# Slot tables read behind the first expert's activation, expert numbers loaded one by one, down biases issued behind the next up

## The chip, the core and the metric

The kernel runs on one core of a Trainium2 chip. Its engines work side by side, each with its own queue in program order: TensorE (PE: matmuls and transposes), VectorE (DVE), ScalarE (ACT), GpSimd (POOL) and SyncE (SP). SP issues the large weight transfers, POOL those with computed row addresses. An instruction starts when those ahead of it on its engine are done and the semaphores it waits for are up. The metric is the device time of one execution in microseconds (us). The kernel before takes 1528.14 us (median of 3 runs, 1527.29 to 1529.5).

## The reference

One decoder layer for 512 tokens of width 1024, in fp32: a normalised input projection feeds a retention and a sliding-window attention group, whose results go through an output projection and are added to `h`. Then comes the part that the change touches, a mixture of experts:

```
logits = xf @ w_router + b_router                 # 512 tokens x 32 experts
top_v, top_i = lax.top_k(logits, 4);  gate = softmax(top_v)
h_e = xblk @ w_up[e] + b_up[e]                    # 1024 -> 2048, tokens grouped by expert
y_e = clamped_swiglu(h_e) @ w_down[e] + b_down[e] # 1024 -> 1024
h   = h + sum over a token's 4 experts of gate * y_e
```

A gated per-layer embedding and a last norm end the layer. Every expert's weights (8 MB up, 4 MB down) are read once; all 32 are used.

## The kernel before

**Routing.** After the router each token has four (expert, position) pairs. Experts are sorted on the chip by their number of tokens and run in a fixed pattern of 32 slots: 20 "L" slots of up to 96 tokens and 12 "S" slots of up to 64, in the order LL SLLSL (five times) SLLLS. For the first two experts `route` (which uses matmuls) builds the row lists at once. For the other thirty, 16 indirect transfers on POOL (L982, four for each of the four tables `slot_d[k]`) scatter token numbers and gates into DRAM, by slot; the table rows are then read back and summed:

```
for k in range(4):                                               # L1005
    nc.gpsimd.dma_start(out=tab[0:CAP, k, :], in_=slot_d[k]...)
R.slots = nc.vector.tensor_reduce(out=slots..., in_=tab...)      # L1006
nc.gpsimd.dma_start(out=slots[64:P, NBIG:E, :], in_=slots[0:64, NBIG:E, :])   # L1008
```

L1009 to L1012 make from it `slot_i`, the row numbers by which `gather` (L798) fetches an expert's tokens and `scatter` (L929) adds its result into `acc`. All this stands in the program between `any_blk` (L1001) and the expert loop.

**Expert loop.** In step e the order of the code is: the gather for expert e+2; `up` or `up64` of expert e (8 pieces of weights); `act` (ACT L885, DVE L886 and L887); the transposes of expert e+1's tokens (`prep` or `prep64`, which make `xTh` and, by DVE L290, `xTl`); `down` of expert e-1 (4 pieces), its gated copy `y` (L924) and its scatter; the transposes of the activation, `act_t` (L901) or `act_t64` (L812). A scheduler orders each engine's queue from this by what is ready; `tc.issue_after(x)` tells it to put an instruction behind `x`.

**L and S.** An L piece (1 MB) is split in two: ACT copies it into `wh` (L150) and DVE subtracts to get `wl` (L151, two operands from SBUF); three products wh·xTh, wh·xTl and wl·xTh (L841) make fp32 precision. An S piece goes to the matmuls unsplit (L858). The bias of a product is a small matmul of its own: `add_bias` (L829) for L, `bias64` (L851) for S. For a down it opens the accumulation.

**Weights.** `next_piece` and `whole_piece` hand out pieces in one fixed order; 12 rotating `raw` tiles hold them, and SP issues the next transfer (L184 up, L189 down) when a tile comes free. Since experts are sorted on the chip, each transfer's address comes from a register, loaded by SP from `eid_i` (`expert_of`, L179). The scheduler put all 30 register loads side by side on SP, ahead of the third up piece.

Of the kernel before, what the change touches and what calls it, by code (L numbers as in the profile page):

```python
# [22 lines left out]
P = 128  # L23
S = 512
NT = S // P
D = 1024
# [69 lines left out]
def hymba_kernel(ctx, tc, x, p, positions, rel_bias_table, g_mix_norm, w_in, b_in, ret_norm_g,  # L96
# [76 lines left out]
    def expert_of(w, t):  # L173

        if t < 2:
            return w[t]
        if t not in R.eid:
            r = RANK[t]
            R.eid[t] = nc.values_load(R.eid_i[0:1, r:r + 1], engines=[mybir.EngineType.SP], min_val=0, max_val=E - 1)  # L179
        return w[bass.ds(R.eid[t], 1)].rearrange("o k c -> (o k) c")  # L180

    def w_up_piece(e, k):
        def load(t):
            nc.sync.dma_start(out=t, in_=expert_of(w_up, e)[k * P:(k + 1) * P, :])  # L184
        return load

    def w_down_piece(e, f):
        def load(t):
            nc.sync.dma_start(out=t.rearrange("p (k c) -> p k c", k=2),  # L189
                              in_=expert_of(w_down, e)[f * 2 * P:(f + 1) * 2 * P, :].rearrange("(k p) c -> p k c", p=P))  # L190
        return load

    def w_proj_piece(t):
# [38 lines left out]
    def whole_piece(use):  # L232

        t, pl_ = queue.pop(0)
        use(t)
        free.append(pl_)
        prefetch()
# [586 lines left out]
    def add_bias(o, e, c0, n, **kw):  # L824

        for c in range(0, n, 512):
            for v in range(2):
                rows = slice(v * 64, v * 64 + 64)
                nc.tensor.matmul(o[v][:, c:c + 512], lhsT=sel[rows, RANK[e]:RANK[e] + 1].broadcast_to([64, P]),  # L829
                                 rhs=R.bias[rows, c0 + c:c0 + c + 512], **kw)  # L830

    def up_tile():
        return R.up.tile([P, 1024], F32, name="up")
# [1 line left out]
    def up(xT, piece, e):  # L835
        h = [up_tile(), up_tile()]
        for k in range(KD):
            wh, wl = piece(k)
            for a, w in ((xT[0], wh), (xT[1], wh), (xT[0], wl)):
                for n in range(4):  # L840
                    nc.tensor.matmul(h[n // 2][:, n % 2 * 512:n % 2 * 512 + 512], lhsT=a[:, k, :],  # L841
                                     rhs=w[:, n * 512:(n + 1) * 512], start=(k == 0 and a is xT[0] and w is wh), stop=False)
        add_bias(h, e, 0, 1024, start=False, stop=True)
        return h

    def bias64(o, e, c0):
# [6 lines left out]
    def pairs64(o, xT, k, w, last):  # L853

        n = w.shape[1] // 2
        for c in range(0, n, 512):
            for v in range(2):
                nc.tensor.matmul(o[v * 64:v * 64 + 64, c:c + 512], lhsT=xT[:, k, :], rhs=w[:, v * n + c:v * n + c + 512],  # L858
                                 start=False, stop=last, tile_position=(0, v * 64))

    def up64(xT, e):
        h = up_tile()
        bias64(h, e, 0)
        for k in range(KD):
            whole_piece(lambda w: pairs64(h, xT, k, w, k == KD - 1))
        return [h]

    def down64(aT, e):
        o = R.dn.tile([P, D], F32, name="dn")[:, 0:512]
        bias64(o, e, 1024)  # L870
        for f in range(4):
            def use(w):
                for kk in range(2):
                    pairs64(o, aT, f * 2 + kk, w[:, kk * D:(kk + 1) * D], f * 2 + kk == KD - 1)
            whole_piece(use)
        return o
# [30 lines left out]

    def down(aT, piece, e):
        o = R.dn.tile([P, D], F32, name="dn")
        add_bias([o[:, 0:512], o[:, 512:D]], e, 1024, 512, start=True, stop=False)  # L910
        for f in range(4):
            wh, wl = piece(f)
            for kk in range(2):
                k = f * 2 + kk
                for a, w in ((aT[0], wh), (aT[1], wh), (aT[0], wl)):
                    for n in range(2):
                        nc.tensor.matmul(o[:, n * 512:(n + 1) * 512], lhsT=a[:, k, :],  # L917
                                         rhs=w[:, kk * 1024 + n * 512:kk * 1024 + (n + 1) * 512],
                                         start=False, stop=(k == KD - 1 and w is wl))
        return o  # L920
# [79 lines left out]
    any_blk = rt.tile([P, 1], I32, name="any_blk")  # L1000
    nc.vector.tensor_copy(out=any_blk, in_=nb_m)  # L1001

    tab = tl.tile([P, 4, 2 * E], F32, name="tab", bufs=1)
    for k in range(4):
        nc.gpsimd.dma_start(out=tab[0:CAP, k, :], in_=slot_d[k].rearrange("(s e) c -> s (e c)", e=E))  # L1005
    R.slots = nc.vector.tensor_reduce(out=slots.rearrange("p e c -> p (e c)")[0:CAP], in_=tab[0:CAP].rearrange("p k f -> p f k"),  # L1006
                                      op=ALU.add, axis=AX.X)
    nc.gpsimd.dma_start(out=slots[64:P, NBIG:E, :], in_=slots[0:64, NBIG:E, :])  # L1008
    nc.vector.tensor_scalar(slot_i[0:CAP, 0:NBIG], slots[0:CAP, 0:NBIG, 0], 512.0, None, op0=ALU.add)  # L1009
    half = tl.tile([P, E], F32, name="cmp", bufs=1)[:, NBIG:E]  # L1010
    nc.vector.tensor_scalar(half, slots[:, NBIG:E, 0], 2.0, 1024.0, op0=ALU.mult, op1=ALU.add)
    nc.vector.tensor_scalar(slot_i[:, NBIG:E], half, cst[:, C_HALF:C_HALF + 1], None, op0=ALU.add)  # L1012
    px.close()

    def open_pools(stack, tag, dn=True):
# [18 lines left out]
    for e in range(E + 1):  # L1034
        if e < E:
            def piece(k, e=e):
                if ahead:
                    return ahead.pop(0)
                with tc.issue_after(R.act.ins) if (e, k) == (1, 2) else nullcontext():
                    return next_piece()  # L1040

            if e + 2 < E:
                static_gather(e + 2)
            h = up(xT, piece, e) if BIG[e] else up64(xT, e)
            a = act(h)
            if e + 1 < E:
                xT = (prep if BIG[e + 1] else prep64)(xe[(e + 1) % 2])
        if e == E - 1:

            last = raw_tile()  # L1050
            aT_last = act_t64(a)
        if e == E:
            tmp = raw_tile()
            p_sb = tmp[0][:, 0:D].rearrange("p (i d) -> p i d", i=NT)
            nc.sync.dma_start(out=p_sb, in_=p.rearrange("(i p) d -> p i d", p=P))
            state["limit"] = n_moe + 3
            for _ in range(3):
                prefetch(after=y)
            ph, pl = halves(raw_tile(F32R)[0], 2)
            for i in range(NT):  # L1060
                split_t(R.tp, p_sb[:, i, :], ph[:, :, i * P:(i + 1) * P], pl[:, :, i * P:(i + 1) * P], n=2)
            aT = aT_last
        if e > 0:
            big = BIG[e - 1]
            y = gated(down(aT, lambda f: next_piece(), e - 1) if big else down64(aT, e - 1), routes[e - 1][1])
            scatter(y, routes[e - 1][0], CAP if big else P, 1 if big else 2)
        if e < E - 1:
            aT = act_t(a) if BIG[e] else act_t64(a)
# [184 lines left out]
```

## Time and profile before

| | |
|---|---|
| median of 3 runs | 1528.14 us |
| profiled execution, its own time | 1529.3 us |
| its span, first to last instruction | 1527.2 us |
| busy: PE, DVE, ACT, POOL | 1379.6, 888.4, 728.7, 209.9 us |
| mean granted TensorE clock | 0.962 of full |
| L150 splits on ACT (267), mean | 1863 ns |
| L151 splits on DVE (267), mean | 2229 ns |
| weights over q1 | 436.24 MB, 73.2% of 16 engines' span |

The span is what the trace covers; the execution's own time is 2.1 us longer. Busy time is a sum over stages: PE is busy for 90% of the span; the experts run from about 303 to 1440 us, and PE stands still from about 307 to 333 us. A time in a row counts from the start of the span.

### The profile page before, as it was taken

The numbers are of one execution on the slowest core, as the hardware profiler recorded it, in microseconds if no ns is written. First come the engines' busy times: TensorE is split into PE (matmuls) and PEld (weight loads), VectorE is DVE, ScalarE is ACT, GpSimd is POOL, SyncE is SP. The second block draws the span as 40 slices with busy tenths as digits, with TensorE's granted clock in tenths as the row PEclk, the third lists the DMA queues.
The fourth block names the chain that finished last, engine by engine and source line by source line (L and its number), as shares of the span: only waits on it lengthen the run. The fifth ranks groups of instructions, "written<-read, shape, count | busy, mean of one in ns | idle before, by whom it ended". The sixth has DMA issues, their size and how long they took to land. (4 is left out here: it accounts for less than half of the span.)

```text
span 1527.2 us, 17227 instructions
## 1 busy us (share of the span) xinstructions
PE 1379.6 (90%) x6208; PEld 939.0 (61%) x6209; DVE 888.4 (58%) x1052; ACT 728.7 (48%) x782; POOL 209.9 (14%) x230
## 2 busy tenths in 40 slices
PE   6998999529999999999999999999999999999785
PEld 4775777427677647656567647656567647675464
DVE  6535674728576537656366627646366537684256
ACT  5333543416465526544455516544355526564343
POOL 2203231450111100000100100000100100000013
PEclk9998999759999999999999999999999999999898
DMA  8422146618899999999999999999999999996601
GB/s 258 136 83 56 36 149 257 235 61 327 328 397 407 380 411 398 407 380 386 397 392 362 375 395 399 403 326 387 395 390 356 375 388 411 387 346 251 215 23 52
DMA packets 110428, 462.49 MB, mean 303 GB/s; under 512 B 10954, under 2 KB 29304, under 8 KB 77568
## 3 DMA queue, kind: packets, MB, share of 16 engines
q1 hardware_dynamic: 99584, 436.24, 73.2%
q0 software_dynamic: 10320, 24.51, 6.3%
q8 instruction: 50, 0.82, 0.2%
q10 hardware_dynamic: 432, 0.57, 0.1%
q14 instruction: 42, 0.34, 0.1%
HBM read 447.53 MB, written 18.99 MB: 305 GB/s over the span
## 5 line engine op out<-in xcount | busy, mean ns | idle before, releaser
L151 DVE TENSOR_TENSOR wl<-raw,wh 128x2048 fp32r<-128x2048 f32 (+2 forms) x267 | 585.4, 2229 | 124.9 <-ACT wh L150 113.7
L150 ACT ACTIVATE wh<-raw 128x2048 fp32r<-128x2048 f32 (+2 forms) x267 | 489.3, 1863 | 129.2 <-PE up L841 90.5
L841 PE MATMUL up<-wh,xTl 128*128 128x512 f32 x640 | 178.3, 400 | 26.7 <-DVE xTl L290 26.7
L841 PE MATMUL up<-wh,xTh 128*128 128x512 f32 x640 | 179.1, 401 | 7.8 <-ACT wh L150 6.3
L841 PE MATMUL up<-wl,xTh 128*128 128x512 f32 x640 | 179.5, 402 | 2.3 <-DVE wl L151 2.3
L858 PE MATMUL up<-raw,xTh 128*64 128x512 f32 x768 | 169.4, 595 | 0.0
L886 DVE TENSOR_SCALAR a<-up 128x512 f32<-128x512 f32 x52 | 34.0, 686 | 232.5 <-ACT sg L885 232.5
L841 PEld LDWEIGHTS up<-wh,xTl 128*128 128x128 f32 x640 | 121.7, 190 | 56.7 <-DVE xTl L290 27.4
L841 PEld LDWEIGHTS up<-wl,xTh 128*128 128x128 f32 x640 | 119.9, 190 | 43.4 <-issue 8.4
L841 PEld LDWEIGHTS up<-wh,xTh 128*128 128x128 f32 x640 | 119.5, 189 | 41.5 <-ACT wh L150 11.6
L798 POOL DMA_INDIRECT xe<-xg,slot_i x30 | 40.6, 1354 | 565.4 <-PE tp L298 317.1
L858 PEld LDWEIGHTS up<-raw,xTh 128*64 128x64 f32 x768 | 53.2, 137 | 103.3 <-issue 98.2
L885 ACT ACTIVATE sg<-up 128x512 f32<-128x512 f32 x52 | 28.9, 598 | 165.7 <-PE up L858 84.2
L917 PE MATMUL dn<-wl,aTh 128*128 128x512 f32 x320 | 103.8, 406 | 4.2 <-DVE wl L151 4.2
L917 PE MATMUL dn<-wh,aTh 128*128 128x512 f32 x320 | 105.6, 412 | 0.3 <-ACT wh L150 0.3
L929 POOL DMA_INDIRECT acc<-y,slot_i x30 | 45.1, 1504 | 419.8 <-ACT y L924 409.8
L917 PE MATMUL dn<-wh,aTl 128*128 128x512 f32 x320 | 102.7, 403 | 0.0
L858 PE MATMUL dn<-raw,aT 128*64 128x512 f32 x384 | 100.1, 601 | 0.0
L924 ACT ACTIVATE y<-dn,slots 128x1024 f32<-128x1024 f32 (+1 forms) x30 | 28.3, 944 | 102.2 <-PE dn L917 81.9
L917 PEld LDWEIGHTS dn<-wl,aTh 128*128 128x128 f32 x320 | 59.8, 192 | 21.0 <-DVE wl L151 8.0
L917 PEld LDWEIGHTS dn<-wh,aTh 128*128 128x128 f32 x320 | 59.5, 193 | 18.9 <-ACT wh L150 2.8
L917 PEld LDWEIGHTS dn<-wh,aTl 128*128 128x128 f32 x320 | 61.5, 192 | 15.0
(338 smaller groups left out, 1566.9 us busy)
## 6 DMA issues: line engine op xcount, KB each, us to landing
raw<-in_w_up_dram SPq DMA_DIRECT2D x256, 1024.0 KB, 11.4
raw<-in_w_down_dram SPq DMA_DIRECT2D x128, 1024.0 KB, 11.0
raw<-in_w_in_dram SPq DMA_DIRECT2D x32, 256.0 KB, 4.8
raw<-in_w_out_dram SPq DMA_DIRECT2D x4, 1024.0 KB, 5.7
raw<-in_w_ple_gate_dram SPq DMA_DIRECT2D x4, 1024.0 KB, 12.4
raw<-in_w_in_dram SPq DMA_DIRECT2D x3, 1024.0 KB, 5.3
xt<-in_x_dram SPq DMA_DIRECT2D x4, 512.0 KB, 7.4
h<-in_x_dram POOLq DMA_DIRECT2D x4, 512.0 KB
```

What stands on the lines that cost most here:

```text
L150: R.split_act = nc.scalar.activation(to(wh), src(raw), AF.Copy)
L151: R.split_dve = nc.vector.tensor_tensor(out=to(wl), in0=src(raw), in1=to(wh).bitcast(F32), op=ALU.subtract)
L798: return nc.gpsimd.indirect_dma_start(out=dst[0:n, 0:D // h], out_offset=None, in_=xg.rearrange("s (h d) -> (s h) d", h=h), in_offset=bass ...
L841: nc.tensor.matmul(h[n // 2][:, n % 2 * 512:n % 2 * 512 + 512], lhsT=a[:, k, :], rhs=w[:, n * 512:(n + 1) * 512], start=(k == 0 and a is x ...
L858: nc.tensor.matmul(o[v * 64:v * 64 + 64, c:c + 512], lhsT=xT[:, k, :], rhs=w[:, v * n + c:v * n + c + 512], start=False, stop=last, tile_p ...
L885: nc.scalar.activation(sg[:, cs], hv[:, :, 0], AF.Silu, scale=ALPHA)
L886: nc.vector.tensor_scalar(a[:, cs], hv[:, :, 1], LIMIT + 1.0, 1.0 - LIMIT, op0=ALU.min, op1=ALU.max)
L917: nc.tensor.matmul(o[:, n * 512:(n + 1) * 512], lhsT=a[:, k, :], rhs=w[:, kk * 1024 + n * 512:kk * 1024 + (n + 1) * 512], start=False, sto ...
L924: nc.scalar.activation(y[:, 0:o.shape[1]], o, AF.Copy, scale=gate)
L929: nc.gpsimd.indirect_dma_start(out=acc.rearrange("s (h d) -> (s h) d", h=h), out_offset=bass.IndirectOffsetOnAxis(ap=idx[0:n, :], axis=0), ...
```

## The change

Three parts. (1) The reading of the slot tables becomes a function `read_slots`, called in step 0 of the expert loop behind `act`; its reduction is put behind the activation's last DVE instruction, `R.act`. The gather for expert 2 moves behind it. Its two scratch tiles are now buffers of the loop's `y`. (2) Each register load of an expert number is put behind the last weight transfer issued before it. (3) The bias matmuls of a down are put behind the last matmul of the up that precedes it in the program (`R.up_end`).

```
@@ expert_of
-            R.eid[t] = nc.values_load(R.eid_i[0:1, r:r + 1], engines=[mybir.EngineType.SP], min_val=0, max_val=E - 1)
+            with tc.issue_after(R.load.ins):
+                R.eid[t] = nc.values_load(R.eid_i[0:1, r:r + 1], engines=[mybir.EngineType.SP], min_val=0,
+                                          max_val=E - 1)
@@ w_up_piece (w_down_piece alike)
-            nc.sync.dma_start(out=t, in_=expert_of(w_up, e)[k * P:(k + 1) * P, :])
+            R.load = nc.sync.dma_start(out=t, in_=expert_of(w_up, e)[k * P:(k + 1) * P, :])
@@ up: add_bias now returns its last matmul
-        add_bias(h, e, 0, 1024, start=False, stop=True)
+        R.up_end = add_bias(h, e, 0, 1024, start=False, stop=True)
@@ up64: pairs64 keeps its last matmul in R.pair
+        R.up_end = R.pair
@@ down64
-        bias64(o, e, 1024)
+        with tc.issue_after(R.up_end.ins):
+            bias64(o, e, 1024)
@@ down
-        add_bias([o[:, 0:512], o[:, 512:D]], e, 1024, 512, start=True, stop=False)
+        with tc.issue_after(R.up_end.ins):
+            add_bias([o[:, 0:512], o[:, 512:D]], e, 1024, 512, start=True, stop=False)
@@ behind any_blk
-    tab = tl.tile([P, 4, 2 * E], F32, name="tab", bufs=1)
-    for k in range(4):
-        nc.gpsimd.dma_start(out=tab[0:CAP, k, :], in_=slot_d[k].rearrange("(s e) c -> s (e c)", e=E))
-    R.slots = nc.vector.tensor_reduce(...)
-    ...
+    def read_slots():
+        tab = R.sb.tile([P, D], F32, name="y")[:, 0:8 * E].rearrange("p (k f) -> p k f", k=4)
+        half = R.sb.tile([P, D], F32, name="y")[:, NBIG:E]
+        for k in range(4):
+            nc.gpsimd.dma_start(out=tab[0:CAP, k, :], in_=slot_d[k].rearrange("(s e) c -> s (e c)", e=E))
+        with tc.issue_after(R.act.ins):
+            nc.vector.tensor_reduce(...)
+        ...
@@ expert loop
-            if e + 2 < E:
+            if 0 < e < E - 2:
                 static_gather(e + 2)
             h = up(xT, piece, e) if BIG[e] else up64(xT, e)
             a = act(h)
+            if e == 0:
+                read_slots()
+                static_gather(2)
```

VectorE's queue from the end of the routing to the second expert's first split, before (`tab` is what POOL reads back from the slot tables; the first `xTl` pair belongs to expert 0, the second to expert 1):

```order
L1001 CAST any_blk<-nb_m 128x1
L1006 TENSOR_REDUCE slots<-tab 96x64
L1009 TENSOR_SCALAR slot_i<-slots 96x20
L1011 TENSOR_SCALAR cmp<-slots 128x12
L1012 TENSOR_SCALAR slot_i<-cmp,cst 128x12
L290 TENSOR_TENSOR xTl<-tp,xTh 128x512 x2
L151 TENSOR_TENSOR wl<-raw,wh 128x2048 x8
L886 TENSOR_SCALAR a<-up 128x512 x2
L887 SCALAR_TENSOR_TENSOR a<-sg,a 128x512 x2
L290 TENSOR_TENSOR xTl<-tp,xTh 128x512 x2
L151 TENSOR_TENSOR wl<-raw,wh 128x2048
L904 SCALAR_TENSOR_TENSOR aTl<-tp,aTh 128x512 x2
```

The same stretch after the change (`y` is the tile into which the tables are now read, and the scratch of L1020):

```order
L1007 CAST any_blk<-nb_m 128x1
L292 TENSOR_TENSOR xTl<-tp,xTh 128x512 x2
L151 TENSOR_TENSOR wl<-raw,wh 128x2048 x8
L891 TENSOR_SCALAR a<-up 128x512 x2
L892 SCALAR_TENSOR_TENSOR a<-sg,a 128x512 x2
L1016 TENSOR_REDUCE slots<-y 96x64
L292 TENSOR_TENSOR xTl<-tp,xTh 128x512
L1019 TENSOR_SCALAR slot_i<-slots 96x20
L292 TENSOR_TENSOR xTl<-tp,xTh 128x512
L151 TENSOR_TENSOR wl<-raw,wh 128x2048
L1020 TENSOR_SCALAR y<-slots 128x12
L909 SCALAR_TENSOR_TENSOR aTl<-tp,aTh 128x512
```

The reduction and the three small instructions behind it moved past expert 0's `xTl`, its eight splits and its activation; they now stand in front of and between the two `xTl` of expert 1.

TensorE's queue at the end of the up of expert 12, an S slot (its products are `up<-raw`; `tp<-cst,a` are the transposes of its activation, the products behind them the down of expert 11, whose bias is `dn<-bias`), before:

```order
L298 MATMUL tp<-cst,xe_2055 128x128 x4
L829 MATMUL dn<-bias,sel 128x512 x2
L858 MATMUL up<-raw,xTh 64x512 x32
L812 MATMUL tp<-cst,a 128x128 x4
L298 MATMUL tp<-cst,xe_2054 128x128
L917 MATMUL dn<-wh,aTh 128x512 x2
L917 MATMUL dn<-wh,aTl 128x512 x2
```

And after the change:

```order
L300 MATMUL tp<-cst,xe_2055 128x128 x8
L861 MATMUL up<-raw,xTh 64x512 x32
L831 MATMUL dn<-bias,sel 128x512 x2
L814 MATMUL tp<-cst,a 128x128 x4
L300 MATMUL tp<-cst,xe_2054 128x128
L923 MATMUL dn<-wh,aTh 128x512 x2
L923 MATMUL dn<-wh,aTl 128x512 x2
```

The two bias matmuls moved from ahead of the 32 up products to behind them, just ahead of the transposes that wait for the activation. In five L slots that follow an L slot (experts 9, 14, 19, 24 and 29) the bias moves in the same way from ahead of the up to behind it; in the S slots 10, 15, 20, 25 and 31 it moves there from the middle of the up. In S slot 5 the transposes of the activation now stand ahead of the down products and not among them. On SP one register load stands ahead of each expert's first piece, where all thirty stood together.

## Rows read from the trace of the kernel before

**Rows 1.** Waits from 307 to 1440 us: total, times, longest.
```profile
PE up L841 <- DVE xTl L290: 26.7, 1, 26.7
...
PE up L841 <- ACT wh L150: 6.3, 5, 1.3
...
PE dn L829 <- ACT y L924: 1.8, 9, 0.2
```

**Rows 2.** Windows: PE, PEld, DVE, ACT, POOL busy; clock; DMA share; GB/s.
```profile
480.00:530.00 50.00, 50.00 (x234) 33.06 (x233) 29.81 (x22) 26.41 (x23) 9.13 (x5) 1.00 1.02 387
...
333.50:337.10 3.60, 3.58 (x9) 2.81 (x9) 2.76 (x2) 1.47 (x1) 1.09 (x1) 0.50 0.23 68
337.10:340.00 2.90, 2.90 (x14) 2.36 (x13) 2.29 (x1) 1.26 (x2) 0.00 (x0) 0.99 0.90 288
```

**Rows 3.** Timeline 300 to 337 us: start, duration, instruction, [idle before <-releaser].
```profile
305.95 1.04 POOL L982 DMA_INDIRECT slot_d<-pay,dest  x1 [7.48 <-DVE dest L979]
...
306.78 0.15 DVE L1001 CAST any_blk<-nb_m 128x1 int32<-128x1 f32 x1
...
325.20 0.97 POOL L982 DMA_INDIRECT slot_d<-pay,dest  x1 [0.30 <-issue]
...
329.83 0.58 DVE L1006 TENSOR_REDUCE slots<-tab 96x64 f32<-96x256 f32 x1 [22.89 <-DMA tab<-slot_d]
330.44 0.17 DVE L1009 TENSOR_SCALAR slot_i<-slots 96x20 int32<-96x20 f32 x1
...
332.77 1.29 DVE L290 TENSOR_TENSOR xTl<-tp,xTh 128x512 fp32r<-128x512 f32 x2
...
333.52 2.07 PE L841 MATMUL up<-wh,xTl 128*128 128x512 f32 x4 [26.68 <-DVE xTl L290]
```

**Rows 4.** Timeline of DVE, 333 to 364 us: expert 0's splits and activation.
```profile
333.98 2.28 DVE L151 TENSOR_TENSOR wl<-raw,wh 128x2048 fp32r<-128x2048 f32 x1
337.58 2.29 DVE L151 TENSOR_TENSOR wl<-raw,wh 128x2048 fp32r<-128x2048 f32 x1 [1.31 <-ACT wh L150]
...
355.13 2.29 DVE L151 TENSOR_TENSOR wl<-raw,wh 128x2048 fp32r<-128x2048 f32 x1 [0.51 <-ACT wh L150]
...
359.61 1.28 DVE L887 SCALAR_TENSOR_TENSOR a<-sg,a 128x512 f32<-128x512 f32 x2
```

**Rows 5.** Timeline of DVE at 385 us.
```profile
385.18 2.29 DVE L151 TENSOR_TENSOR wl<-raw,wh 128x2048 fp32r<-128x2048 f32 x1 [0.51 <-ACT wh L150]
```

**Rows 6.** Timeline of POOL at 385 us.
```profile
385.64 2.66 POOL L798 DMA_INDIRECT xe<-xg,slot_i  x1 [25.80 <-PE tp L812]
```

**Rows 7.** Timeline of all engines, 796 to 798 us.
```profile
796.06 1.59 POOL L929 DMA_INDIRECT acc<-y,slot_i  x1 [0.31 <-issue]
796.40 2.29 DVE L151 TENSOR_TENSOR wl<-raw,wh 128x2048 fp32r<-128x2048 f32 x1 [2.92 <-ACT wh L150]
```

**Rows 8.** Timeline of POOL, 290 to 300 us.
```profile
293.43 2.78 POOL L798 DMA_INDIRECT xe<-xg,idx  x1 [0.85 <-DVE idx L793]
```

**Rows 9.** Timeline of PE, 293 to 340 us.
```profile
301.76 0.90 PE L298 MATMUL tp<-cst,xe 128*128 128x128 f32 x3 [8.45 <-DMA xe<-xg,idx]
```

**Rows 10.** Timeline of PE, 660 to 752 us.
```profile
669.47 0.49 PE L829 MATMUL dn<-bias,sel 64*128 64x512 f32 x2
669.90 7.09 PE L858 MATMUL up<-raw,xTh 128*64 128x512 f32 x32
...
693.20 1.10 PE L841 MATMUL up<-wh,xTh 128*128 128x512 f32 x4
...
745.78 0.66 PE L812 MATMUL tp<-cst,a 128*128 128x128 f32 x4 [2.67 <-DVE a L887]
```

**Rows 11.** Line 179: durations ns, first and last start.
```profile
L179 SPq TENSOR_LOAD <-eid_i x30: 1/262/1112, 303.8 to 328.0; - x30
```

**Rows 12.** Line 184: time of its transfers from issue to landing.
```profile
DMA to landing us min/median/max: 4.7/11.4/21.5
```

**Rows 13.** Timeline of SP, 660 to 690 us.
```profile
663.11 14.25 SPq L184 DMA_DIRECT2D raw<-in_w_up_dram  x8
```

More of the change, by code (lines that the diff above doesn't have):

```diff
@@ L188, in load @@
         def load(t):
-            nc.sync.dma_start(out=t.rearrange("p (k c) -> p k c", k=2),
-                              in_=expert_of(w_down, e)[f * 2 * P:(f + 1) * 2 * P, :].rearrange("(k p) c -> p k c", p=P))
+            src = expert_of(w_down, e)[f * 2 * P:(f + 1) * 2 * P, :].rearrange("(k p) c -> p k c", p=P)
+            R.load = nc.sync.dma_start(out=t.rearrange("p (k c) -> p k c", k=2), in_=src)
         return load
@@ L828, in add_bias @@
                 rows = slice(v * 64, v * 64 + 64)
-                nc.tensor.matmul(o[v][:, c:c + 512], lhsT=sel[rows, RANK[e]:RANK[e] + 1].broadcast_to([64, P]),
-                                 rhs=R.bias[rows, c0 + c:c0 + c + 512], **kw)
+                m = nc.tensor.matmul(o[v][:, c:c + 512], lhsT=sel[rows, RANK[e]:RANK[e] + 1].broadcast_to([64, P]),
+                                     rhs=R.bias[rows, c0 + c:c0 + c + 512], **kw)
+        return m
     def up_tile():
@@ L857, in pairs64 @@
             for v in range(2):
-                nc.tensor.matmul(o[v * 64:v * 64 + 64, c:c + 512], lhsT=xT[:, k, :], rhs=w[:, v * n + c:v * n + c + 512],
-                                 start=False, stop=last, tile_position=(0, v * 64))
+                R.pair = nc.tensor.matmul(o[v * 64:v * 64 + 64, c:c + 512], lhsT=xT[:, k, :],
+                                          rhs=w[:, v * n + c:v * n + c + 512], start=False, stop=last, tile_position=(0, v * 64))
     def up64(xT, e):
@@ L1001, in hymba_kernel @@
     nc.vector.tensor_copy(out=any_blk, in_=nb_m)
-    tab = tl.tile([P, 4, 2 * E], F32, name="tab", bufs=1)
-    for k in range(4):
-        nc.gpsimd.dma_start(out=tab[0:CAP, k, :], in_=slot_d[k].rearrange("(s e) c -> s (e c)", e=E))
[L1006 to L1012, printed above, removed]
+    def read_slots():
[4 more added lines that the diff above has]
+        with tc.issue_after(R.act.ins):
+            nc.vector.tensor_reduce(out=slots.rearrange("p e c -> p (e c)")[0:CAP], in_=tab[0:CAP].rearrange("p k f -> p f k"),
+                                    op=ALU.add, axis=AX.X)
+        nc.gpsimd.dma_start(out=slots[64:P, NBIG:E, :], in_=slots[0:64, NBIG:E, :])
+        nc.vector.tensor_scalar(slot_i[0:CAP, 0:NBIG], slots[0:CAP, 0:NBIG, 0], 512.0, None, op0=ALU.add)
+        nc.vector.tensor_scalar(half, slots[:, NBIG:E, 0], 2.0, 1024.0, op0=ALU.mult, op1=ALU.add)
+        nc.vector.tensor_scalar(slot_i[:, NBIG:E], half, cst[:, C_HALF:C_HALF + 1], None, op0=ALU.add)
     px.close()
```

## The prediction, made before the changed kernel ran

> **What bounds the kernel now.** I began with the waits of the expert stage. TensorE has one that stands far above the others: 26.7 us, once, before the product `up<-wh,xTl` of the first expert, for VectorE's `xTl` [rows 1]. The windows then tell what bounds the rest: in a stretch in the middle of the experts PE is busy for all of 50 us at a granted clock of 1.00 [rows 2]. DMA is as full there, but weights come early: the first up piece of expert 11 is issued at 663.11 and its first product starts at 693.20, 30.1 us later [rows 10, 13], where the slowest of all up transfers took 21.5 us to land and the median 11.4 [rows 12]. So PE paces the experts, and a hole in PE is worth its length.
>
> The timeline shows what fills the 26.7 us [rows 3]. VectorE is done with `any_blk` at 306.93 and stands in front of the reduction of the slot tables until 329.83. Behind it in VectorE's queue is `xTl` of expert 0, which needs nothing of the tables but starts at 332.77; PE goes on at 333.52. The tables are late because POOL issues 16 scatters one after the other, 0.97 us and a gap of 0.30 each, from 305.95 to 326.17, and the tables are read back and land 3.66 us after that.
>
> **Part 1, what goes.** With the reduction out of the way `xTl` follows `any_blk` at 306.95 instead of 332.77: everything from there on moves up by 25.82 us. TensorE is cold on both sides: its granted clock was 0.50 of full (1.2 GHz) until 337.1 after the stall [rows 2], and I keep the same for the new start. Gain 25.8.
>
> **Part 1, what is late next.** The reduction now stands behind expert 0's activation and, in VectorE's queue, in front of expert 1's `xTl`, for which PE will wait as it did before. VectorE is free for it when the second half of the activation ends, at 359.61 + 1.28 = 360.89 before [rows 4], 335.07 after the shift. With scatters as fast as before the tables would land at 329.83 and nothing would wait. But the 16 scatters now run beside expert 0's eight splits, which they did not before. A POOL transfer that begins in a split is held: the gather that starts at 385.64, inside a split that ends at 387.47, ends at 388.30, 0.83 us after the split [rows 5, 6]. I let every scatter that begins in a split end 0.83 us behind it. The shifted splits start at 308.16, 311.76, 315.3 and then every 2.80 us (2.29 + 0.51) up to 329.31 [rows 4]. Scatter 2 ends at 308.3, still as before. Scatter 3 is held to 311.27; the gaps ahead of splits 2 and 3 are wide enough for one scatter to slip in front of each (4 and 6), so 5 and 7 are held by splits 2 and 3. From there a scatter ends 0.83 and the next begins 1.13 us after a split's end, when the next split has run for 0.6 us: one scatter per split, and scatter 12 ends 0.83 after the last split's end at 331.60, at 332.43. Scatter 13 is free (332.73 to 333.70), 14 begins in the second activation instruction, which also reads two operands from SBUF, and ends at 335.90, 15 at 337.17, 16 at 338.44. That is 12.3 us later than before. The tables land 3.66 us later, at 342.1: VectorE waits 7.0, and with the reduction (0.58) and the counterpart of L1009 (0.17) expert 1's `xTl` is 7.8 us late. Loss 7.8.
>
> The bounds of this term: no hold at all, 0.75 us (the two instructions alone). Above: the scatters as worked out, but the last one and the read behind it landing as slowly as a gather beside weight traffic, which took from 293.43 to 301.76, 8.33 us [rows 8, 9]: 337.47 + 2 x 8.33 = 354.1, so 19.0 + 0.75 = 19.8 us late. I stay near 7.8 because SP issues a transfer only when a tile comes free: while PE pauses, none does, the weight transfers under way end, and the reads should land nearly as in the quiet rows.
>
> After such a pause PE is cold again. The 3.58 us of work until 337.1 [rows 2] would have taken half at full clock: loss 1.7 to 1.8, I take 1.7 (0 without a pause, twice that if the clock stays low as long again). The second scratch step (L1020) waits for a copy between partitions, which with the instruction around it took 332.77 - 330.41 = 2.36 us before [rows 3]; a split of 2.28 us now stands ahead of it. I take 0.3, between 0 and 2.4. The gathers for experts 2 and 3 start some 10 us later than the shift alone would put them, but are wanted only at the end of expert 1's up, eight pieces of 2.80 us later: nothing.
>
> What follows in POOL's and SP's queues: on POOL the reads have only long finished work ahead besides the scatters; the first `y` copy needs the two scratch buffers, free long before expert 0's down is done. Nothing.
>
> **Part 2, register loads.** The thirty loads ran on SP from 303.8 to 328.0 [rows 11], 24.2 / 29 = 0.83 us each, inside the stall. With the stall gone they would have stood in front of the next weight piece; now each stands in front of one expert's first piece. One such stop delays a piece by up to 1.1 us (the longest load) that is issued 30.1 us before its use and takes at most 21.5 us to land: still 8.6 us to spare. Nothing, as long as a stop stays below that.
>
> **Part 3, biases.** In ten S slots the two bias matmuls (669.47 to 669.90, 0.43 us [rows 10]) move from a busy place into the hole ahead of the transposes of the activation, which lasts 2.67 us and is VectorE's and ScalarE's [rows 10]: 10 x 0.43. In five of these the bias stood first in the up and also waited for the gated copy of the expert before, 0.2 each (1.8 us in all, nine times [rows 1]): 5 x 0.20. In five L slots it moves out of a hole: the up that follows waits for ScalarE's split, up to 1.3 us a time [rows 1], so it was free there and costs 0.43 at the end of the up: -2.2. In S slot 5 transposes now wait ahead of the down products that used to cover them: at most 2.67 - 0.43 = 2.2, I take half, -1.1. Sum 4.3 + 1.0 - 2.2 - 1.1 = +2.0 gain. Shorter holes may also spare PE some falls of its clock, or other holes cause some: -2 to +6.
>
> **Sum.** -25.8 + 7.8 + 1.7 + 0.3 - 2.0 = -18.0 us. The profiled execution took 1529.3 (span 1527.2 and 2.1 around it), so 1511.3; it lies 1.2 above the median of the runs, and from the median of 1528.14 I forecast 1510.1.
>
> **Rivals.**
> A. POOL is not held. For it: a split did not suffer from a scatter that began 0.34 us before it (2.29 us long as ever [rows 7]), so the two can overlap, and the held gather is a single one and no scatter. Against: the 0.83 us behind a split's end [rows 5, 6]. The loss shrinks to 0.75, no pause, no cold restart: -25.8 + 0.75 - 2.0 = -27.0, 1501.
>
> B. Most of the stall only moves. The scatters are held and the last landings are slow: the upper bound above, 19.8 late: -25.8 + 19.8 + 1.7 + 0.3 - 2.0 = -6.0, 1522. For it: transfers on POOL do land late beside weights [rows 8, 9]; against: the weight queue is empty in the pause.
>
> C. The lock works both ways. A scatter that starts first would hold the split for up to 0.97 us; the splits have 0.51 us to spare, so up to 0.46 us for each of eight pieces, 3.7 in all: 1513.8. The Trainium skill, page "SBUF — State Buffer", section "SBUF: two separate sides", says that a VectorE instruction with two SBUF inputs and a GpSimd one that reads SBUF share a port pair, and that whichever starts first keeps it for its whole length while the other is blocked. For the split that starts first the trace agrees (0.83 us behind its end); for POOL first it does not, as the split at 796.40 ran its usual 2.29 us beside the scatter from 796.06 to 797.65 [rows 7]. By the page's rule the time would be the 1513.8, by the trace it stays at 1510.1.
>
> D. Slower than before: the stops on SP. A register load stands in the queue in front of weights, and its time was only ever seen while SP had nothing else to do. If such a stop, with the address work behind it, lasts d beside a full DMA, each of 30 experts starts late by d - 8.6: it decides from d = 8.6, eats the gain from 8.6 + 18.0 / 30 = 9.2, and at d = 10 costs 42 us: 1552. Against: the longest load was 1.1 us.
>
> **How the numbers follow.** The forecast gets 0.5, A 0.15, B 0.2, C 0.1, D 0.03; 0.02 is left for the change not doing what its order says. The likeliest case's own range is 1505 to 1515 (a piece of the scatter count either way, the bias term from -2 to +6). For 8 in 10 I go from 1499 (A with the upper end of the bias term cut off) to 1519 (most of B). A measurement of this kernel can tell about 0.2%, 3 us, from no change: faster needs less than 1525.1, which the forecast, A, B and C give; B's worse corner and half of the rest may fall within 0.2%: 0.95 faster, 0.02 the same, 0.03 slower (D).
>
> **What the profile after would show.** `xTl` of expert 0 right behind `any_blk`, and no wait of PE over 1 us there. Scatters up to about 2.5 us long between 308 and 332, one per split, the last ending near 338; if they stay at 0.97, A. The reduction waiting some 7 us for the read (15 or more: B), and PE about as long, with a clock of 0.50 for 3 to 4 us behind it. Splits of 2.29 us beside scatters (longer or starting later: C). One load per expert on SP and no wait of ACT or PE for weights (else D). The hole before the transposes of S slots with the bias in it, some 2.2 us instead of 2.7. The prediction is wrong if the median is above 1519 or below 1499.

## The result, and the profile after

The changed kernel takes 1501.41 us (median of 4 runs, 1498.92 to 1502.44), the kernel before in runs beside it 1528.56 us (1527.29 to 1529.5): a ratio of 0.982, 95% interval 0.9804 to 0.9835. The forecast was 1510.1 with a range of 1499 to 1519: the time is in it, but the gain is 27 us where 18 were forecast.

The profiled execution of the changed kernel took 1498.9 us with a span of 1496.8, 30.4 less than the one before, so the comparison of the two traces is over 30.4 us. Of the page, first the stall. The timeline of the changed kernel (start, duration, instruction, idle before and its releaser) has these in the place of [rows 3]:

```profile
306.43 0.15 DVE L1007 CAST any_blk<-nb_m 128x1 int32<-128x1 f32 x1
...
306.64 1.29 DVE L292 TENSOR_TENSOR xTl<-tp,xTh 128x512 fp32r<-128x512 f32 x2
...
307.39 2.07 PE L844 MATMUL up<-wh,xTl 128*128 128x512 f32 x4 [0.90 <-DVE xTl L292]
...
311.28 0.97 POOL L988 DMA_INDIRECT slot_d<-pay,dest  x1 [0.30 <-issue]
...
311.44 2.29 DVE L151 TENSOR_TENSOR wl<-raw,wh 128x2048 fp32r<-128x2048 f32 x1 [1.31 <-ACT wh L150]
...
318.82 2.29 DVE L151 TENSOR_TENSOR wl<-raw,wh 128x2048 fp32r<-128x2048 f32 x1 [0.51 <-ACT wh L150]
...
319.46 2.49 POOL L988 DMA_INDIRECT slot_d<-pay,dest  x1 [0.30 <-issue]
...
333.30 1.29 DVE L891 TENSOR_SCALAR a<-up 128x512 f32<-128x512 f32 x2 [0.98 <-ACT sg L890]
333.46 0.97 POOL L988 DMA_INDIRECT slot_d<-pay,dest  x1 [0.30 <-issue]
...
337.94 0.97 POOL L988 DMA_INDIRECT slot_d<-pay,dest  x1 [0.64 <-DMA slot_d<-pay,dest]
...
342.60 0.58 DVE L1016 TENSOR_REDUCE slots<-y 96x64 f32<-96x256 f32 x1 [6.81 <-DMA y<-slot_d]
...
343.84 1.12 PE L906 MATMUL tp<-cst,a 128*128 128x128 f32 x4 [8.36 <-DVE xTl L292]
```

`xTl` follows `any_blk` at once, and PE idles 0.90 us where it idled 26.68. The scatters beside the splits end 0.84 us behind the split (319.46 + 2.49 = 321.95, the split ends at 321.11). The one at 333.46, which begins beside the first half of the activation, takes 0.97 us as if alone. The last one ends at 338.91, the reduction waits 6.81 us for the tables, and PE has a new hole of 8.36 us ahead of expert 1. TensorE comes out of it cold: in the window behind the hole the granted clock (seventh figure) is at its half level for most of the time.

```profile
344.50:348.00 3.50, 3.50 (x14) 2.92 (x13) 3.50 (x5) 1.65 (x3) 3.03 (x2) 0.59 0.10 20
```

The waits of PE behind 307 us, for [rows 1] (total, times, longest): one long wait of 26.7 us has become one of 8.4, the hole ahead of an S slot's transposes has shrunk to 2.3, and the waits for ScalarE's splits are more and longer (15 where there were 5).

```profile
PE tp L814 <- DVE a L892: 24.2, 11, 2.3
...
PE up L844 <- ACT wh L150: 11.6, 15, 2.0
...
PE tp L906 <- DVE xTl L292: 8.4, 1, 8.4
```

How far PE is ahead of the trace before, at the end of the same matmuls in both timelines:

| last matmul of | before | after | ahead by |
|---|---|---|---|
| up of expert 0 | 356.9 | 331.8 | 25.1 |
| down of expert 0 | 396.6 | 381.1 | 15.45 |
| up of expert 5 | 508.1 | 492.7 | 15.45 |
| up of expert 6 | 545.7 | 532.5 | 13.2 |
| down of expert 31 | 1429.2 | 1399.5 | 29.6 |

So the stall brings 25.1 and gives 9.7 back, close to what was worked out; experts 5 and 6 lose 2.3; and from there to the end some 16.4 us are gained, where the prediction had 2.0 for all of part 3. Waits cannot be their source: in that stretch (545.7 to 1429.2 us before, 532.5 to 1399.5 after) PE idles 42.9 us before and 43.1 after, while its busy time falls from 840.7 to 824.0; over the whole span it falls from 1379.6 to 1364.4 us with the same 6208 matmuls. In the groups of the page (busy, mean ns of one) the kernel before has

```profile
L858 PE MATMUL up<-raw,xTh 128*64 128x512 f32 x768 | 169.4, 595 | 0.0
...
L858 PE MATMUL dn<-raw,aT 128*64 128x512 f32 x384 | 100.1, 601 | 0.0
```

and the kernel after

```profile
L861 PE MATMUL up<-raw,xTh 128*64 128x512 f32 x768 | 168.3, 594 | 0.0
...
L861 PE MATMUL dn<-raw,aT 128*64 128x512 f32 x384 | 88.3, 598 | 0.0
```

The products of the S downs take 11.8 us less. In the stretch behind expert 6 it is 10.7, where no other group falls by more than 2.2 (the transposes of tokens). Each lasts the same (601 and 598 ns), but their sum, in which what overlaps counts once, is 260 ns a record before and 230 after, where the ups of the same shape have 220. The timeline suggests why, and e9 and e10 test it. An S product fills 64 of the 128 columns (`tile_position`), and two neighbours, left and right half, run side by side. The trace counts each product as two records. Expert 10's down before:

```profile
715.69 1.07 PE L858 MATMUL dn<-raw,aT 128*64 128x512 f32 x2
716.69 1.20 PE L841 MATMUL up<-wl,xTh 128*128 128x512 f32 x4
717.83 0.73 PE L829 MATMUL up<-bias,sel 64*128 64x512 f32 x4
718.48 3.65 PE L858 MATMUL dn<-raw,aT 128*64 128x512 f32 x14
```

and after:

```profile
702.84 5.37 PE L861 MATMUL dn<-raw,aT 128*64 128x512 f32 x24
...
709.40 1.94 PE L861 MATMUL dn<-raw,aT 128*64 128x512 f32 x8
```

Before, one product (2 records) slipped into the end of the up, and it took 1.00 us alone; its partner stood behind the up, and so another one was left over at the end of the 7 products (14 records) that followed: five turns of about 0.85 us for eight products instead of four. In the changed kernel the bias, which opens the accumulation, waits for the end of the up, so no product can slip in front of it, and the runs are 12 and 4 products long: whole pairs.

SP now loads the expert numbers one by one over the whole stage. A load takes 0.27 us (median), as it did before (0.26); the 0.83 us of the prediction was the distance between loads, not their length [rows 11]:

```profile
L180 SPq TENSOR_LOAD <-eid_i x30: 263/274/297, 327.2 to 1320.3; - x30
```

### The profile page after: what moved, and what is told of

The parts are those of the page before. It is cut to its first block, busy times and chain, and to the rows that moved or that the text cites. A ratio compares the mean times of both kernels' runs of the same rounds, so it can differ in the third digit from the quotient of the medians.

```text
span 1496.8 us, 17238 instructions
## 1 busy us (share of the span) xinstructions
PE 1364.4 (91%) x6208; PEld 939.3 (63%) x6209; DVE 886.2 (59%) x1052; ACT 728.4 (49%) x782; POOL 224.7 (15%) x230
## 5 line engine op out<-in xcount | busy, mean ns | idle before, releaser
L800 POOL DMA_INDIRECT xe<-xg,slot_i x30 | 42.9, 1429 | 370.8 <-PE tp L814 222.1
L861 PE MATMUL dn<-raw,aT 128*64 128x512 f32 x384 | 88.3, 598 | 0.0
```

Of the source, the lines that this page charges most:

```text
L800: return nc.gpsimd.indirect_dma_start(out=dst[0:n, 0:D // h], out_offset=None, in_=xg.rearrange("s (h d) -> (s h) d", h=h), in_offset=bass ...
L861: R.pair = nc.tensor.matmul(o[v * 64:v * 64 + 64, c:c + 512], lhsT=xT[:, k, :], rhs=w[:, v * n + c:v * n + c + 512], start=False, stop=las ...
```

## The experiments

My theory: (T1) the stall is worth 15.4 us, 25.1 less what the held scatters give back; (T2) the rest comes from whole pairs in ten S downs. Each time below is a median beside the kernel before on the same chip.

**e1: part 3 alone.** The edits of `up`, `up64`, `pairs64`, `down64` and `down` from the diff above, on the kernel before.

> The kernel before with part 3 alone (down biases behind the next up). My theory: what was gained outside the stall, about 14 us, comes from TensorE's order alone: ten S downs lose their split into 1 + 7 or 11 products, which broke a pair of column halves (10 x 0.84 = 8.4 us), the switches around it (about 2 us) and the bias in the hole (3 us). Then 1528.6 - 14 = 1514 to 1515. Rival: that gain comes from the earlier start or from SP's loads, and the biases bring the 2.0 us of the prediction: 1526 to 1527.

Measured: 1519.07 us, ratio 0.9915 (0.9889 to 0.994), 12 us gained where 14 were expected; the rival's 2 are out. The page's row for the S downs reads 88.3 us, as in the kernel after. Outside the stall part 3 brings most of the gain. The hole of expert 0 and the loss at experts 5 and 6 are not there, so the 2.3 us go with part 1 (e2 has the loss without part 3).

**e2: parts 1 and 2 without part 3.**

```
-        with tc.issue_after(R.up_end.ins):
-            bias64(o, e, 1024)
+        bias64(o, e, 1024)
```

(and the same in `down`)

> The kernel after without part 3 (biases as before; slot tables late, loads one by one). Theory: the stall alone, 25.1 us gained and 9.7 given back at expert 1, so 15.4 us: 1513. Rival (the rest comes from the earlier start or from the loads): 1503 to 1504.

Measured: 1519.40 us, ratio 0.9929 (0.9905 to 0.9953), 12.1 us gained. The S downs cost 100.1 us, as before. The rival is out; the theory had 3 us too much. At the end of expert 0's down PE is 17.1 us ahead of before, at the end of expert 31's 11.5: the trace loses 3.5 us at expert 5, and its clock fell nine times to the half level in the experts, not seven. So T1 holds for the stall itself, and some of it is lost later.

**e3: only the products.** The bias of an S down where it was, its products behind the next up.

```
         bias64(o, e, 1024)
+        end = R.up_end
...
-                for kk in range(2):
-                    pairs64(o, aT, f * 2 + kk, ...)
+                with tc.issue_after(end.ins):
+                    for kk in range(2):
+                        pairs64(o, aT, f * 2 + kk, ...)
```

> The kernel before, with the products of an S down put behind the last matmul of the next up, and its bias left where it was. Theory: the pairs are whole again (12 and 4 products), 8.4 us for the pairs and up to 2.3 for the switches: 1518 to 1520. Rival: what counts is the place of the bias itself: 1528.

Measured: 1513.87 us, ratio 0.9889 (0.9862 to 0.9916): 17.6 us, more than part 3 as a whole. Its page has the S downs at the same 88.3 us:

```profile
L859 PE MATMUL dn<-raw,aT 128*64 128x512 f32 x384 | 88.3, 598 | 0.0
```

So the place of the biases, from which the prediction took its 2.0 us, brings nothing that shows; what came is the products' order. That e3 is some 5 us faster than e1 goes with the clock: in the experts behind 400 us it stands at its half level for 17 us in e3's trace and for 27 in e1's, which is worth 5 us. Why is not shown.

**e4: without part 2.**

```
-            with tc.issue_after(R.load.ins):
-                R.eid[t] = nc.values_load(...)
+            R.eid[t] = nc.values_load(...)
```

> The kernel after without part 2: all thirty register loads stand together on SP again, ahead of the third piece of the run. Theory: they now keep SP from issuing the pieces of 310 us until about 328, 18 us; the pieces lead their use by 10 us at the least around expert 7, DMA is full there and does not catch up, so PE loses up to 7 us: 1502 to 1509. Rival, as the prediction has it (loads cost nothing): 1501, within 1 us of after.

Measured: 1499.31 us, ratio 0.9786 (0.9762 to 0.9811): no slower than the kernel after. The 18 us did not come about, because the loads do not stand together: with the stall gone the scheduler itself put ten of them at 307 to 313 us and the others later.

```profile
L179 SPq TENSOR_LOAD <-eid_i x30: 261/268/468, 307.6 to 1324.5; - x30
```

Part 2 is worth nothing here, and ten loads in a row cost nothing either. What thirty loads in one block would cost without the stall was not tried.

**e5: pairs in another order.** In the first half piece of each S down the four products in the order left, left, right, right; nothing between them.

```
+        for kk, v in ((0, 0), (1, 0), (1, 1), (0, 1)):
+            nc.tensor.matmul(o[v * 64:v * 64 + 64, 0:512], lhsT=xT[:, k0 + kk, :], ..., tile_position=(0, v * 64))
```

> The kernel after, with the four products of the first half piece of each of the 12 S downs in the order left, left, right, right, left/right swapped (no other instruction between them): the pairs of column halves are broken without any switch to another kind of product. Theory (a broken pair costs the time of one product, 0.84 us): 12 x 0.84 = 10.1 us more than after, 1511. Rival (what cost time in the kernel before was the switch between kinds of products, not the pair): 1501, as after.

Measured: 1501.71 us, ratio 0.9818 (0.9802 to 0.9835): no change against the kernel after. At expert 10 the first 24 records of the down, the eight in the new order ahead, last 5.38 us together; in the kernel after it was 5.37.

```profile
704.20 1.95 PE L859 MATMUL dn<-raw,aT 128*64 128x512 f32 x8
705.97 3.61 PE L867 MATMUL dn<-raw,aT 128*64 128x512 f32 x16
```

The theory as I had put it (neighbours in the wrong order run alone) falls. Left are two readings of the kernel before: the cut itself costs, by its switches, or a product costs that the cut leaves without a partner. e9 and e10 tell these apart.

**e9 and e10: a cut at half a pair, a cut at a whole pair.** One matmul over all columns, with zero weights, behind the third (e9) or the fourth (e10) product of each S down.

```
+                if zero is not None and 2 * k + v == 3:     # 4 in e10
+                    nc.tensor.matmul(o, lhsT=zero, rhs=R.bias[:, 1024:1536], start=False, stop=False)
                 R.pair = nc.tensor.matmul(...)
```

> The kernel after, with one matmul over the full width (weights zero) set into each of the 12 S downs behind its third product, so behind half a pair. Theory (a product that another kind cuts off from its partner in the other column half runs alone, for the time of a pair): on each side of the cut one product runs alone, 0.84 us more per down than with the cut at a whole pair, 12 x 0.84 = 10 us over e10: with about 0.5 us for the matmul itself 1517. Rival (a cut costs the switch, wherever it is): as e10, 1507.

> The same with the matmul behind the fourth product, between two whole pairs. Both theories: after plus 12 times the added matmul and its two switches, about 0.5 us each: 1507.

Measured: e9 1518.60 us, ratio 0.9905 (0.9869 to 0.994); e10 1508.85 us, ratio 0.985 (0.9819 to 0.9882). The same added matmul at the odd place costs 9.8 us more, 0.81 us for each of 12 downs, where 10 us were expected. PE's timeline at expert 10's down, e9 first:

```profile
706.95 1.93 PE L863 MATMUL dn<-raw,aT 128*64 128x512 f32 x6
708.81 0.50 PE L862 MATMUL dn<-bias,zero 128*128 128x512 f32 x1
709.24 4.50 PE L863 MATMUL dn<-raw,aT 128*64 128x512 f32 x18
```

```profile
706.72 1.94 PE L863 MATMUL dn<-raw,aT 128*64 128x512 f32 x8
708.58 0.50 PE L862 MATMUL dn<-bias,zero 128*128 128x512 f32 x1
709.02 3.65 PE L863 MATMUL dn<-raw,aT 128*64 128x512 f32 x16
```

Three products (6 records) take as long as four (8 records), 1.93 and 1.94 us, and nine as long as ten would. T2 holds in this form: a product that another kind of matmul cuts off from its partner takes the time of a pair. On the page the products' row is 9.3 us higher in e9 than in e10:

```profile
L863 PE MATMUL dn<-raw,aT 128*64 128x512 f32 x384 | 100.3, 601 | 0.0
```

```profile
L863 PE MATMUL dn<-raw,aT 128*64 128x512 f32 x384 | 91.0, 601 | 0.0
```

The ten cuts of the kernel before, one turn of 0.85 us each, are 8.5 of the 11.8 us. Most of the rest can be put down to the switches: twelve cuts at whole pairs raise the row by 2.7 us (91.0 against 88.3 in the kernel after), so ten by about 2.2, an estimate.

**e6: one operand.** All eight of expert 0's splits on VectorE as a product of one operand with a constant (expert 0's low parts are left out). The expectation below speaks of the last six; the first two, at 293 and 294 us, were changed too.

```
+                R.split_dve = nc.vector.tensor_scalar(to(wl), src(raw), 0.5, None, op0=ALU.mult)
```

> The kernel after, with the last six splits of expert 0 on VectorE as a product of one SBUF operand with a constant instead of the difference of two (expert 0's low parts are wrong; same tiles and shapes). Theory (a split holds the scatters because it reads two operands from SBUF): scatters beside them last 0.97 us, the tables are there before expert 0's activation is done, TensorE's 8.4 us hole and its cold restart go: 1491 to 1493. Rival (any VectorE instruction from SBUF to SBUF holds them): scatters of 2 to 2.5 us as after, 1498 to 1501.

Measured: 1494.36 us, ratio 0.9773 (0.9757 to 0.9789). The time is near that of the theory, but the trace says something else:

```profile
312.10 1.74 POOL L992 DMA_INDIRECT slot_d<-pay,dest  x1 [0.30 <-issue]
312.50 1.23 DVE L153 TENSOR_SCALAR wl<-raw 128x2048 fp32r<-128x2048 f32 x1 [1.53 <-PE up L848]
...
315.30 1.23 DVE L153 TENSOR_SCALAR wl<-raw 128x2048 fp32r<-128x2048 f32 x1 [1.57 <-PE up L848]
...
315.42 1.94 POOL L992 DMA_INDIRECT slot_d<-pay,dest  x1 [0.30 <-issue]
...
334.83 0.58 DVE L1020 TENSOR_REDUCE slots<-y 96x64 f32<-96x256 f32 x1 [1.49 <-DMA y<-slot_d]
...
336.06 0.86 PE L910 MATMUL tp<-cst,a 128*128 128x128 f32 x4 [3.03 <-DVE xTl L296]
```

The scatter that began in a one-operand split is held too, to 317.36, 0.83 us behind the split's end at 316.53, as with two operands. The scatter at 312.10 is held although it began 0.40 us before its split: it ends at 313.84, 0.11 us behind the split. Two more (at 305.56 and 317.67) do the same, while in the kernel after the scatter that began 0.16 us before a split of two operands was not held. So two operands are not needed for a hold. Whether they are what holds beside the full split stays open, since the split of e6 is another instruction that runs in about half the time. Nor does every VectorE instruction hold: the scatter at 333.46 of the kernel after began in one that reads its operand from `up`, the output of matmuls, and took 0.97 us.

PE's hole falls from 8.36 to 3.03 us, but not by the shorter splits alone. The 16 scatters take 25.5 us from the first start to the last end, where they took 33.3. They also start 5.6 us earlier (300.02 against 305.61), as the routing, in which two of the changed splits stand, ends earlier in this run; and expert 0's up ends 2.5 us earlier. Against that, 9.3 us pass from the last scatter to the reduction, where 3.7 did, with weight transfers on the way. So the 7 us between e6 and the kernel after are not the price of the hold.

**e7: the reduction later.** Behind the split of expert 1's third piece.

```
-        with tc.issue_after(R.act.ins):
+        with tc.issue_after(R.split_dve.ins):
             nc.vector.tensor_reduce(...)
...
+                if (e, k) == (1, 2):
+                    read_slots()
+                    static_gather(2)
+                    static_gather(3)
```

> The kernel after, with the table reduction behind the split of expert 1's third piece instead of behind expert 0's activation. Theory (only the place of the waiting reduction in VectorE's queue makes the 8.4 us hole): TensorE has three split pieces, 8.4 us of work, to go on with; hole under 2 us, no cold restart: 1491 to 1493. Rival (the reads are held by expert 1's splits in turn and the wait moves to expert 1's fourth piece or to the gather of expert 2): 1497 to 1501.

Measured: 1495.49 us, ratio 0.9777 (0.9755 to 0.9799), 0.4% below the kernel after by intervals that just miss each other, taken in different comparisons. In the trace:

```profile
338.23 1.88 POOL L988 DMA_INDIRECT slot_d<-pay,dest  x1 [0.85 <-DMA slot_d<-pay,dest]
...
344.66 1.02 POOL L1014 DMA_DIRECT2D y<-slot_d  x2 [2.13 <-DMA slot_d<-pay,dest]
...
347.19 0.58 DVE L1016 TENSOR_REDUCE slots<-y 96x64 f32<-96x256 f32 x1 [6.72 <-DMA y<-slot_d]
...
350.02 2.07 PE L844 MATMUL up<-wl,xTh 128*128 128x512 f32 x4 [3.07 <-DVE wl L151]
```

The reduction starts 4.6 us later than in the kernel after. Of these, 1.3 us are a later end of the routing in this run (`any_blk` at 307.76 against 306.43). About 1.1 come from the scatters, of which the one at 338.23 is held by expert 1's third split. The remaining 2.1 are the reads: no split runs beside them, but two wait 2.13 us for scatters to land, with weights on the way. PE has work until 346.95, waits 3.07 us and is cold again (0.50 in the four microseconds behind it):

```profile
350.00:354.00 4.00, 3.98 (x9) 3.14 (x10) 3.96 (x5) 1.92 (x1) 2.84 (x2) 0.50 0.77 254
```

The hole shrinks, as in the theory; the wait moves to expert 1's fourth piece, as in the rival, but late landings did more to the reads than a split did. By its median it is the fastest complete version of this study, though its interval and that of e4 overlap.

**e8, e11, e12: covering the hole of the S slots.** On e7, the transposes of an S slot's activation behind the first eight products of the down (e8); besides, one (e11) or two (e12) pieces of that down split ahead of the activation. In all three the down bias of an L slot followed by an L slot is back ahead of the up.

```
+            first = [next_piece()] if not BIG[e] and e < E - 1 else []    # e11; two pieces in e12
...
-            aT = act_t(a) if BIG[e] else act_t64(a)
+            with tc.issue_after(R.down1.ins) if not BIG[e] else nullcontext():
+                aT = act_t(a) if BIG[e] else act_t64(a)
```

> e7 and, besides, in S slots the transposes of the activation behind the first eight of the down's products, which cover the 2.3 us hole, and the down bias of an L slot followed by an L slot back ahead of the up. Theory (TensorE alone paces the experts): e7's time less 10 x 2.3 for the holes and 5 x 0.43, and up to 10 us of clock falls that follow such holes: 1456 to 1468. Rival (with 30 us taken out the weights become the pace): 1475 to 1482, with waits for raw.

> e8, and in S slots also the split of the down's first piece ahead of the activation on ScalarE and VectorE, which are idle before it. Theory (in e8 the first down product took over the wait, 3.1 us ten times, because its split stood behind the activation on ScalarE): the hole goes, 10 x 2.3 us less than e7 and fewer clock falls: 1460 to 1473. Rival (another wait ends last there, or weights become the pace): 1485 to 1500.

> e11 with two pieces of the down split ahead of the S slot's activation instead of one. Theory (in e11 the wait went on to the down's second piece, whose split stands behind the activation on ScalarE, 2.4 us ten times): two pieces are 5.6 us of products and cover activation and third split; the ten holes go, 20 to 25 us less than e7: 1470 to 1478. Rival (three buffers of split pieces do not let the third split start in time, so the wait goes on to the third piece, or ScalarE and VectorE fall behind for the next up): 1495 to 1515.

Measured: e8 1525.87 us (0.9971, 0.9957 to 0.9985), e11 1515.67 us (0.9893, 0.9853 to 0.9933), e12 1516.88 us (0.9896, 0.9869 to 0.9922): all clearly slower than e7 and above what theory and rival had for them (e12 by 2 us, the others by more). PE's hole stays and only changes its owner. PE's waits behind 350 us in e8, then in e12:

```profile
PE dn L923 <- ACT wh L150: 30.3, 11, 3.1
```

```profile
PE dn L923 <- ACT wh L150: 24.1, 10, 2.9
```

In e12's timeline what delays the split stands at the head of ScalarE's queue:

```profile
726.28 1.08 ACT L291 ACTIVATE xTh<-tp 128x512 fp32r<-128x512 f32 x2 [14.27 <-PE up L861]
...
727.26 3.71 ACT L150 ACTIVATE wh<-raw 128x2048 fp32r<-128x2048 f32 x2
...
729.22 0.80 PE L923 MATMUL dn<-wh,aTh 128*128 128x512 f32 x2 [2.61 <-ACT wh L150]
```

ScalarE waits with `xTh` of the next expert for the end of the S up, which still reads the only `xTh` buffer, and the splits stand behind it. I took its idle time for free time. But the waits do not make e12 slower than e7: from 350 us to the end of the experts PE waits 49 us in e12 and 48 in e7. Its busy time grows, from 1368.0 to 1390.1 us with the same 6208 matmuls, and that goes with the clock: over 700 to 750 us it is 0.93 in e12 where e7 has 1.00, and over the whole span 0.950 where e7 has 0.967. As an estimate, that is 0.034 x 1517 = 52 us more at the half level, 26 us of work, more than the 21 us between the two. In the experts behind 400 us e7's clock falls seven times for 3.4 us each, e12's fourteen times, eight of them for 6.8. Why it falls more often was not tried.

```profile
700.00:750.00 50.00, 46.71 (x207) 25.89 (x206) 19.35 (x16) 20.07 (x21) 4.12 (x3) 0.93 1.00 399
```

A second `xTh` buffer, which would show whether that queue makes the wait, was not tried.

## Why the prediction was right where it was, and wrong where not

- **What bounds the kernel** was read rightly: the hole in PE was worth its length, and PE's list of waits shows none for weights, before or after.
- **Part 1, what goes** (25.8): PE's first product behind the stall is 26.1 us ahead (307.39 against 333.52), the end of expert 0's up 25.1. The prediction kept the same cold start for both; after the change the clock stays at its half level for 5.8 us (to 313.2) and not 3.6, which is about the 1.0 that is lost.
- **Part 1, what is late next** (7.8 late): the scatters were to end at 338.44 and end at 338.91, the tables at 342.1 and the reduction starts at 342.60, VectorE was to wait 7.0 and waits 6.81. The reads landed as in the quiet rows, as the prediction argued against B (3.7 us from the last scatter to the reduction); in e6 and e7, with weights on the way, it was 9.3 and 5.8. With the cold restart (1.7) the working has 9.8 given back (0.3 of it for L1020's wait, which does not show); measured 9.7. One name was wrong: of the eight splits in that stretch six are expert 0's and two expert 1's, since the first pieces are split earlier. Scatter 14 was held about as long as forecast (to 336.03 against 335.90); whether by the two operands that were named as the reason, e6 leaves open.
- **Rival A** forecast 1501, which is what was measured, but its mechanism is refuted: the scatters were held. A time that fits does not make the reason right. That the measured time lies in the range is partly luck as well: the lower end, 1499, was drawn from A, while the 9 us below the forecast came from a term that the prediction did not have.
- **Rival C**, the lock that works both ways: the scatter at 311.28 began 0.16 us before the split at 311.44, which ran its 2.29 us all the same. The rule of the Trainium skill, page "SBUF — State Buffer", section "SBUF: two separate sides", that whichever starts first blocks the other, holds here for the split that starts first and not for the scatter. The same section of the Trainium skill has a second case, a VectorE instruction in a mode with two ports. The split of e6 fits that case in so far as it held the scatters and took 1.23 us, about half of 2.29; no run shows that it ran in such a mode. There, too, a scatter that started first did not keep its time (the one at 312.10).
- **Part 2** (nothing): right, and e4 shows it, though the spare lead from which it was argued was hardly tested: the scheduler would have spread most of the loads anyhow.
- **Part 3, biases** (+2.0) is the step that failed. It priced the bias matmuls in their new places and left out what stands behind a bias: the products that accumulate on it. Keeping them behind the up joined the cut pairs, 11.8 us on the page's row for the S downs; part 3 alone brought 12 (e1) where 2.0 were forecast. e3 shows that gain without a move of any bias, and e9 against e10 its mechanism. The terms that I did price: ten holes fell from 2.67 to 2.33, where 0.43 each was forecast; the five L slots' waits for ScalarE grew from 1.3 to 2.0, and ten new ones of 0.2 came; S slot 5's loss, 1.1 in the sum, was 2.3 and goes with part 1. The row that could have told stood on the page before: 100.1 us for 384 records of the down's products, 260 ns each, against 220 ns for the 768 of the up, at the same shape.

What stays open: nearly 6 us of the 16.4 that were gained behind expert 6 (16.4 less the 10.7 of the S downs in that stretch). They are spread over many groups: transposes 2.7, L downs 2.8 and ups 2.3 us less, biases 2.3 more. The clock falls at different places in every trace, seven times in the experts before and six after, and one fall more or less is 1.7 us (3.4 us at the half level). Why PE's order at expert 5 changed with part 1 was not tried either.

## What to carry to other kernels

When an instruction is moved, price also what cannot start without it: a bias that opens an accumulation drags every product of that accumulation along. Where half-width products run in pairs, divide a group's busy time by its count and compare it with a group of the same shape; a higher figure means pairs that are cut, and an odd run on either side of another matmul costs a whole turn. A wait that is moved away from the path comes back at the next instruction in the same queue: ask for the moment at which the data is there, by the slowest transfer beside the new neighbours, and put work for that long in front.

## What the runs showed of the hardware

- A half-width product without a partner takes the time of two: three products 1.93 us, four 1.94 (e9, e10); the order of left and right within a run does not matter (e5).
- A scatter of the slot tables (0.97 us by itself), issued by GpSimd in the midst of a VectorE split, ends about 0.83 us behind the split, with one operand from SBUF as with two (e6 and the kernel after). A split that begins during a scatter is not held (2.29 us beside the scatter at 311.28). Nor is such a scatter, beside a split of two operands; beside one of one operand a scatter that began 0.40 us before it was held to 0.11 us behind its end (312.10 in e6).
- With waits of the same length in sum (49 and 48 us), a kernel can be slower through the clock alone: e12's mean granted clock of 0.950 against e7's 0.967 is worth some 26 us by estimate, and its time is 21 us longer.
